# Masked-autoencoder loss: the first four target columns by three transfers in place of two

## The chip, the cores and the metric

The kernel runs on one core of one Trainium2 chip. The metric is the device time of one execution in microseconds (us). Of several executions the median is given, and one execution is taken by the hardware profiler. In the profile PE is TensorE (matrix multiply), PEld its weight loads, DVE is VectorE, ACT is ScalarE, POOL is GpSimd and SP is SyncE. SP and POOL issue the transfers here (DMA); 16 DMA engines move the data.

## The reference

There are 32 images of 147 masked patches, each patch with 768 numbers, in `pred` and in `target`, both float32. Each target patch is normalised by its own mean and variance, and the mean squared difference to the prediction is taken for each image.

```python
mean = target.mean(axis=-1, keepdims=True)
var = target.var(axis=-1, keepdims=True)
target = (target - mean) / np.sqrt(var + 1e-6)
loss = np.mean((pred - target) ** 2, axis=-1)   # (32, 147)
return loss.mean(axis=-1)                        # (32,)
```

## The kernel before

**Tiling.** Partition `p = 4 b + j` holds a run of consecutive patches of image `b`: `j` runs from 0 to 3 and picks one of four runs of 37 patches (36 real ones in the last run, `KJ` = 37, `KM` = 36). A "column" `c` is one patch of each partition, 128 x 768 numbers. Columns 0 to 35 exist on all 128 partitions. Column 36, called `REST`, exists only for three of the four runs and is a tile of 96 partitions. Since the patches of one run lie one behind the other in memory, a transfer of columns 0 to 3 moves one contiguous piece of 4 x 768 x 4 = 12,288 bytes for each partition.

**Loads.** A list `stream` names all loads in the order in which they are wanted. Columns 0 to 3 of the target and then `REST` of the target are marked `hw`: SP issues them, and they stay float32. All other pieces are marked `sw`: POOL issues them, and they are cast to bfloat16 on the way. Target and prediction pieces alternate in the POOL queue. Each tile is used once, so no load waits for a buffer; but a load from POOL reuses the completion semaphore of the load eight places before it and waits for that one. The function `load` (line 111 for the changed transfers, line 115 for all others) issues one entry of the list. The tile of columns 0 to 3 is filled by two transfers of 64 partitions: one takes the even partitions (`til[0::2]`, the runs `j` = 0 and 2), the other the odd ones.

**Work on a column.** VectorE computes the statistics of a target column (`bn_stats` twice for 384 numbers each, line 165, and `bn_aggr`, line 166). For a group of one to four columns ScalarE takes the root of the variance and the negative mean (lines 189 and 190), and VectorE the reciprocal (line 195). POOL then normalises the column into a bfloat16 tile `s` (line 215). The difference is either made on TensorE, by adding -1 x `s` and 1 x `pred` in PSUM with identity matrices (line 232), and squared with a sum on ScalarE (line 261); or it is made on VectorE (line 277) and squared there (line 281) or on ScalarE (line 261). At the end small matmuls with masks (line 342) add the partial sums of the partitions of each image into `acc`, which is copied (line 373) and stored (line 374).

**Order.** The order on each engine is written out by a planner in the kernel: it keeps a list of operations with an engine, an estimated duration, needs and earliest times, and picks the next one greedily. It works at build time and knows a load only as one operation on SP or POOL of 0.6 us; how many transfers `load` makes of it is not visible to it. The issue instructions are pinned in program order. The engines then run by semaphores alone.

Of the kernel before, what the change touches and what calls it, by code (L numbers as in the profile page):

```python
# [14 lines left out]
def kernel(  # L15
# [8 lines left out]
    pin = tc.keep_in_program_order  # L24
    B, N, D = pred.shape
    eps = 1e-6
    P = 128
    J = P // B
    KJ = (N + J - 1) // J
# [10 lines left out]
    def rows_of(c):  # L40
        return RP if c == REST else P
# [59 lines left out]
    def load(kind, c0, c1, d0, d1, q):  # L101
        x = targ_f if kind == "t" else pred_f
        n, w = rows_of(c0), d1 - d0
        til = data.tile([P, (c1 - c0) * w], BF16 if q == "sw" else F32, name=f"{kind}{c0}_{d0}")
        src = bass.AP(tensor=x.tensor, offset=x.offset + c0 * D + d0,
                      ap=[[N * D, B], [KJ * D, J - 1 if c0 == REST else J], [1, (c1 - c0) * w]])
        eng = {"hw": nc.sync, "hw2": nc.scalar, "sw": nc.gpsimd}[q]
        if c0 == 0 and q == "hw":

            for j in (0, 1):  # L110
                pin(eng.dma_start(out=til[j::2], in_=bass.AP(  # L111
                    tensor=x.tensor, offset=src.offset + j * KJ * D,
                    ap=[[N * D, B], [2 * KJ * D, J // 2], [1, (c1 - c0) * w]])))
        else:
            pin(eng.dma_start(out=til[:n], in_=src))  # L115
        for c in range(c0, c1):
            KIND[kind].setdefault(c, []).append((d0, d1, til, (c - c0) * w))
# [3 lines left out]
    for i, (kind, c0, c1, d0, d1, q) in enumerate(stream):  # L121
        w = (c1 - c0) * (d1 - d0)
        clock += w * rows_of(c0) / P * 0.915 / D + (0.0 if w >= 4 * D else 0.04)
        lanes[q].append(clock + 1.1)
        for c in range(c0, c1):
            land[kind, c, d0] = clock + 1.1
        k = len(lanes[q])
        op(("load", i), {"hw": "SP", "hw2": "ACT", "sw": "POOL"}[q], 0.6, [], lambda a=stream[i]: load(*a), rank=-1.0,
           early=0.0 if k <= 8 else lanes[q][k - 9] + 0.3)
# [164 lines left out]
    for k, (u, d0, d1, eng) in enumerate(units):  # L294
        w = len(u) * (d1 - d0)
# [40 lines left out]
        out=rl_sum, in_=rl, axis=mybir.AxisListType.X, op=ALU.add)), rank=3.0)  # L336
# [73 lines left out]
```

## Time and profile before

| | us |
|---|---|
| median of 4 runs | 76.79 |
| lowest and highest | 76.45, 77.25 |
| the profiled execution | 76.45 |
| its span, first to last instruction | 74.7 |

| engine | busy us | share of the span |
|---|---|---|
| VectorE | 55.9 | 75% |
| GpSimd | 52.6 | 70% |
| ScalarE | 31.0 | 41% |
| TensorE | 26.9 | 36% |

The POOL queue moved 13.52 MB as the profile counts them (bytes written, which are half the bytes read because of the cast), SP's queue 1.87 MB. The times in the profile's views are microseconds from the start of the span. A line number is that of the kernel before. In the chain of work that ended last, each entry names what the next one was released by; "SPq" is the sequencer of SP, and "issue" is time in which nothing shown was waited for. In a table of stretches, each engine's busy time is followed by its number of instructions, and the last columns are the granted TensorE clock, the mean busy share of the 16 DMA engines and the rate in GB/s. A transfer is counted in the stretch where its packets start, so a share can be over 1.

### The profile page before, as it was taken

How to read it: one execution, taken by the hardware profiler on the slowest of the kernel's cores; microseconds unless marked ns; L12 is line 12 of the kernel's file. 1: busy time of each engine (PE TensorE's matmuls, PEld its weight loads, DVE VectorE, ACT ScalarE, POOL GpSimd, SP SyncE). 2: the span in 40 equal slices, each digit the busy share in tenths (PEclk: the TensorE clock that was granted, in tenths of full speed). 3: DMA queues.
4: the chain of work that ended last, by engine and by line, in shares of the span. 5: the costliest groups of instructions: out<-in, count | busy, mean ns of one | idle time of the engine just before them, and what ended most of it. 6: DMA issues, size and time to landing. Idle time of an engine off the chain costs nothing.

```text
span 74.7 us, 563 instructions
## 1 busy us (share of the span) xinstructions
PE 26.9 (36%) x88; PEld 8.2 (11%) x88; DVE 55.9 (75%) x154; ACT 31.0 (41%) x67; POOL 52.6 (70%) x72
## 2 busy tenths in 40 slices
PE   0000003470000000498940004978860720578750
PEld 0000000110000000123300001222320300112120
DVE  0000899999999979990899999860997579999870
ACT  5100022202002020069502020598969979988960
POOL 5899008996199929699869993994799799960000
PEclk9999999999999999999999855589999998555895
DMA  0899999999999999999999989999999999999900
GB/s 0 191 428 355 260 217 214 195 223 224 240 217 210 210 198 211 234 217 210 230 217 224 217 185 214 211 217 214 217 214 220 197 212 212 215 204 206 168 1 0
DMA packets 3269, 15.41 MB, mean 206 GB/s; under 512 B 386, under 2 KB 1122, under 8 KB 2754
## 3 DMA queue, kind: packets, MB, share of 16 engines
q0 software_dynamic: 2992, 13.52, 88.7%
q1 hardware_dynamic: 274, 1.87, 7.0%
q14 instruction: 3, 0.02, 0.1%
HBM read 28.90 MB, written 0.00 MB: 387 GB/s over the span
## 4 chain that ended last, share of the span: by engine, by line
DMA 72%; DVE 10%; POOL 10%; issue 2%; ACT 1%; PE 1%; SPq 1%; ACTq 0%; POOLq 0%; DVEq 0%
DMA p<-in_pred_dram 63%; POOL s L215 9%; DMA t<-in_target_dram 8%; DVE st L165 6%; DVE zd L277 2%; DVE mv L166 1%; SPq L111 1%; ACT zp L261 1%; POOL p L115 1%; PE zp L232 1%; PE acc L342 0%; ACT r L189 0%; DVE ob L373 0%; DVE r L195 0%; ACTq L405 0%
## 5 line engine op out<-in xcount | busy, mean ns | idle before, releaser
L215 POOL TENSOR_SCALAR s<-t,nm,r 128x768 bf16<-128x768 bf16 (+2 forms) x37 | 39.2, 1066 | 6.9 <-DVE r L195 6.4
L165 DVE BATCH_NORM_STATS2 st<-t 128x6 f32<-128x384 bf16 (+2 forms) x74 | 36.2, 530 | 8.1 <-DMA t<-in_target_dram 8.1
L232 PE MATMUL z<-p,ident 128*128 128x512 bf16 (+2 forms) x26 | 9.5, 504 | 21.7 <-DMA p<-in_pred_dram 21.7
L189 ACT ACTIVATE r<-mv,eps_t 128x4 f32<-128x4 f32 (+2 forms) x11 | 3.2, 295 | 31.0 <-DVE mv L166 30.2
L261 ACT ACTIVATE z<-z 128x1536 f32<-128x1536 f32 (+1 forms) x9 | 12.3, 1364 | 8.1 <-PE z L232 8.1
L232 PE MATMUL z<-s,nident 128*128 128x512 bf16 (+2 forms) x26 | 10.1, 504 | 15.2 <-POOL s L215 13.9
L115 POOL DMA_DIRECT2D p<-in_pred_dram x15 | 8.6, 572 | 6.1 <-DMA t<-in_target_dram 4.1
L277 DVE TENSOR_TENSOR zd<-p,s 128x1536 bf16<-128x1536 bf16 (+4 forms) x13 | 8.7, 689 | 2.0 <-DMA p<-in_pred_dram 1.8
L166 DVE BATCH_NORM_AGGREGATE mv<-st 128x2 f32<-128x12 f32 (+1 forms) x37 | 7.7, 209 | 1.3
L232 PEld LDWEIGHTS <-ident 128*128 128x128 bf16 (+1 forms) x36 | 4.4, 122 | 35.6 <-issue 34.0
L261 ACT ACTIVATE zd<-zd 128x1536 bf16<-128x1536 bf16 (+1 forms) x5 | 6.7, 1348 | 0.7 <-DVE zd L277 0.5
L232 PEld LDWEIGHTS <-nident 128*128 128x128 bf16 (+1 forms) x36 | 3.4, 111 | 27.3 <-issue 14.9
L281 DVE SCALAR_TENSOR_TENSOR zd<-zd 128x512 bf16<-128x512 bf16 (+3 forms) x8 | 5.4, 680 | 0.2
L195 DVE RECIPROCAL r<-r 128x4 f32<-128x4 f32 (+2 forms) x11 | 1.5, 133 | 4.0 <-ACT r L189 4.0
L232 PE MATMUL zp<-p,ident 128*128 128x512 bf16 x5 | 2.4, 561 | 4.8 <-DMA p<-in_pred_dram 4.8
L115 POOL DMA_DIRECT2D t<-in_target_dram x6 | 3.6, 624 | 0.0
L261 ACT ACTIVATE zl<-zl 128x512 f32<-128x512 f32 (+1 forms) x5 | 2.8, 563 | 0.4 <-PE zl L232 0.3
L261 ACT ACTIVATE zp<-zp 128x1024 f32<-128x1024 f32 (+1 forms) x3 | 2.6, 865 | 0.3 <-PE zp L232 0.2
L232 PE MATMUL zp<-s,nident 128*128 128x512 bf16 x5 | 1.6, 427 | 2.5 <-ACT z L261 2.5
L232 PE MATMUL zl<-p,ident 128*128 128x512 bf16 (+1 forms) x5 | 2.2, 500 | 0.7 <-DMA p<-in_pred_dram 0.7
L232 PE MATMUL zl<-s,nident 128*128 128x512 bf16 (+1 forms) x5 | 1.9, 420 | 0.4 <-POOL s L215 0.4
L190 ACT ACTIVATE nm<-mv 128x4 f32<-128x4 f32 (+2 forms) x11 | 2.1, 189 | 0.0
(29 smaller groups left out, 10.7 us busy)
## 6 DMA issues: line engine op xcount, KB each, us to landing
t<-in_target_dram POOLq DMA_DIRECT2D x4, 768.0 KB, 13.4
t<-in_target_dram POOLq DMA_DIRECT2D x2, 1536.0 KB, 27.1
p<-in_pred_dram POOLq DMA_DIRECT2D x4, 768.0 KB, 38.4
t<-in_target_dram SPq DMA_DIRECT2D x2, 768.0 KB, 5.5
p<-in_pred_dram POOLq DMA_DIRECT2D x1, 1536.0 KB, 39.0
p<-in_pred_dram POOLq DMA_DIRECT2D x4, 384.0 KB, 29.9
p<-in_pred_dram POOLq DMA_DIRECT2D x3, 192.0 KB, 15.7
t<-in_target_dram SPq DMA_DIRECT2D x1, 288.0 KB, 8.1
```

The lines of the kernel that those rows point to most:

```text
L111: pin(eng.dma_start(out=til[j::2], in_=bass.AP(tensor=x.tensor, offset=src.offset + j * KJ * D, ap=[[N * D, B], [2 * KJ * D, J // 2], [1, ...
L115: pin(eng.dma_start(out=til[:n], in_=src))
L165: pin(nc.vector.bn_stats(out=st[:n, j, :], in_=x))
L166: pin(nc.vector.bn_aggr(out=out, in_=st[:n, :len(parts)]))
L189: pin(nc.scalar.activation(out=r[:n], in_=mv[:n, :, 1], func=ACTF.Sqrt, bias=eps_t[:n], scale=1.0))
L190: pin(nc.scalar.activation(out=nm[:n], in_=mv[:n, :, 0], func=ACTF.Copy, scale=-1.0))
L195: pin(nc.vector.reciprocal(out=rs[g][:n], in_=rs[g][:n]))
L215: pin(nc.gpsimd.tensor_scalar(out=s[:n, so:so + D], in0=til[:n, o:o + D], scalar1=nm, scalar2=r, op0=ALU.add, op1=ALU.mult))
L232: pin(nc.tensor.matmul(z[:n, zo + a:zo + b], eye[:n, :n], src[:n, o + a:o + b], start=first, stop=not first))
L261: pin(nc.scalar.activation(out=z[:n, :w], in_=z[:n, :w], func=ACTF.Square, accum_out=dest[:n]))
L277: pin(nc.vector.tensor_tensor(out=x, in0=y, in1=v, op=ALU.subtract))
L281: pin(nc.vector.scalar_tensor_tensor(out=z, in0=z, scalar=1.0, in1=z, op0=ALU.mult, op1=ALU.mult, accum_out=dest))
```

## The change

The tile of columns 0 to 3 is filled by three transfers: 32 partitions (every fourth, from 0: run `j` = 0), then 64 partitions (the odd ones: runs 1 and 3), then 32 partitions (every fourth, from 2: run `j` = 2). Each partition is still one piece of 12,288 bytes, and the tile, its consumers and all other loads are unchanged. SP issues the three transfers and then `REST`, four in place of three. The consumers of the tile (line 165 on VectorE and line 215 on POOL) wait for three completion semaphores in place of two.

```diff
         if c0 == 0 and q == "hw":
 
-            for j in (0, 1):
-                pin(eng.dma_start(out=til[j::2], in_=bass.AP(
+
+            for j, step in ((0, 4), (1, 2), (2, 4)):
+                pin(eng.dma_start(out=til[j::step], in_=bass.AP(
                     tensor=x.tensor, offset=src.offset + j * KJ * D,
-                    ap=[[N * D, B], [2 * KJ * D, J // 2], [1, (c1 - c0) * w]])))
+                    ap=[[N * D, B], [step * KJ * D, J // step], [1, (c1 - c0) * w]])))
```

The change adds one line to the file, so lines after it have a number higher by one in the kernel after.

## The prediction

> **What bounds the kernel now.** I read the chain that ended last first, then the page's slices and totals, then stretches of the trace at the start and at the end, and last the instructions of the first microseconds.
>
> The chain that ended last, merged, in order of time (start us, us, what):
>
> ```profile
> 0.81 0.63 SPq L111
> 1.45 0.06 issue
> 1.50 6.16 DMA t<-in_target_dram
> 7.66 0.03 issue
> ...
> 16.57 39.92 DMA p<-in_pred_dram
> ...
> 63.61 7.46 DMA p<-in_pred_dram
> 71.07 0.04 issue
> 71.12 0.39 PE zp L232
> ...
> 72.59 0.18 DVE ob L373
> ```
>
> The reader is to see that 72% of the chain is DMA, and that its head is the pair of transfers that is changed: the second is issued at 1.45 and lands at 7.66, and only then does VectorE begin. From this alone one would say that the start of VectorE sets the end, and that is the reading to distrust. The page says what the transfer engines did meanwhile:
>
> ```profile
> DMA  0899999999999999999999989999999999999900
> HBM read 28.90 MB, written 0.00 MB: 387 GB/s over the span
> ```
>
> They are 90% busy or more from the third slice to the thirty-eighth. The stretches at both ends (columns: five engines, granted clock, DMA share, GB/s written):
>
> ```profile
> 2.00:2.20 0.20, 0.00 (x0) 0.06 (x1) 0.00 (x0) 0.09 (x1) 0.17 (x1) 1.00 0.00 0
> 2.20:2.40 0.20, 0.00 (x0) 0.00 (x0) 0.00 (x0) 0.00 (x0) 0.13 (x2) 1.00 3.44 614
> ...
> 4.00:6.00 2.00, 0.00 (x0) 0.00 (x0) 0.00 (x0) 0.00 (x0) 2.00 (x5) 1.00 0.96 406
> ...
> 68.00:70.00 2.00, 2.00 (x6) 0.56 (x5) 1.82 (x8) 1.77 (x6) 0.00 (x0) 0.58 1.16 204
> 70.00:71.00 1.00, 0.47 (x2) 0.10 (x1) 0.86 (x5) 0.88 (x5) 0.00 (x0) 1.00 0.93 134
> 71.00:72.00 1.00, 0.82 (x13) 0.38 (x12) 0.93 (x4) 0.94 (x3) 0.00 (x0) 1.00 0.02 2
> ```
>
> Data first moves at 2.2 and stops at 71.1: 68.9 us for 28.90 MB, 419 GB/s, next to 406 GB/s in the stretch 4 to 6, where plain f32 copies alone run (GpSimd's transfers write bf16, so half of what they read). The stream never pauses for long, so the end is the moment its first byte moves, plus a fixed amount of work, plus 3.6 us of tail. VectorE's head can slip without moving the end so long as GpSimd issues its transfers early enough: its last issue, at 66.01, lands some 5 us later behind transfers already queued. VectorE itself waits 0.52 us at 27.85 and 0.78 us at 49.18 for target data, and 2.0 us twice for ScalarE. So what the change is worth is what it does to the start of the stream.
>
> **What the Trainium skill says.** "DMA: Bandwidth & Descriptors", Why a DMA increments its semaphore by 16 and not by 1: the engines used are the largest number up to 16 that divides the slowest dimension of both access patterns. 64 rows and 32 rows both give 16, four rows and two rows to an engine; the 406 GB/s agrees for 64, and no run yet shows 32. Same page, Queues, rings and completion order: an engine alternates between the queues that have work, packet by packet. The trace agrees: SP's transfers have the engines alone at first (406 GB/s), then the written rate falls to 316 in 6 to 8 and to 240 in 8 to 10, when GpSimd's come in. Same page, Rules for kernel authors: two transfers to disjoint halves of the partitions share the same engines and run one after the other; by this a third gains no bandwidth. Same page, Latency and other measured facts: first byte after about 0.6 us for this path; here the first data moves 1.4 us after the issue begins at 0.81, or 0.8 after it ends.
>
> **The change part by part.**
>
> ```profile
> 0.81 1.27 SPq L111 DMA_DIRECT2D t<-in_target_dram  x2
> 2.13 0.61 SPq L115 DMA_DIRECT2D t<-in_target_dram  x1
> 3.10 1.24 POOL L115 DMA_DIRECT2D t<-in_target_dram  x2
> ...
> 7.76 1.02 DVE L165 BATCH_NORM_STATS2 st<-t 128x6 f32<-128x384 f32 x2 [6.82 <-DMA t<-in_target_dram]
> ```
>
> (1) One more issue on SP. A 64-row issue takes 0.58 or 0.63 us and the 96-row one 0.61; only the single row of the output takes less (0.29). So the price hardly follows the rows, and a 32-row issue is taken at 0.6: the three start near 0.81, 1.4 and 2.05, and the transfer of the last column group (line 115), queued behind them on SP, moves from 2.13 to 2.7. SP has nothing else until the output. GpSimd's queue is not touched: its first issue stays at 3.10.
>
> (2) The same 128 rows of 12,288 bytes in a new order. At 406 GB/s over 16 engines a row takes 0.48 us. The packet records show 0.46 in steady flow, and 0.85 to 1.34 for each engine's very first row. Bytes and rows per engine (8) are as before, so the flow costs nothing more. The added semaphore writes, one per engine, take 0.01 us each in those records.
>
> (3) Does the ring run dry behind a first transfer of only two rows per engine? First data at 2.23, two rows of about 1.1 and 0.46: needed again at 3.8. The second transfer is issued at 1.4 and, with the same 1.42 us to first data, is ready at 2.85: 0.95 us early. The third, issued at 2.05, is ready at 3.5 and needed at 3.8 + 4 x 0.46 = 5.6. The last group: ready at 4.1, needed at 6.5, when the before trace's first rows of it move. All three are covered by data in flight; the loss is 0. If the cover were gone, each late 0.1 us would be 0.1 us at the end, since the stream bounds it.
>
> (4) The start of the first data. This is the one term that can move the end. With everything fixed per instruction the gain is 0. The upper end: the output's one row needs about 0.73 us from issue to its packet, against 1.42 for the 64 rows; if all 0.69 of the difference were in proportion to the rows, half the rows would save 0.35. Issues of 64 and 96 rows cost the same, which speaks for the fixed kind, so I take 0.1.
>
> (5) The waits. VectorE's first statistics and GpSimd's first normalisation wait for three semaphores in place of two; a queue step of this kind is 0.02 us in the chain, and behind VectorE's wait stands its whole sequence, which has slack as shown. The order of instructions on VectorE, ScalarE, TensorE and GpSimd is the same, because the planner sees one load as before.
>
> The sum: 0.1 off the stream's start, some 0.02 on the wait, so 0.1 off the end. The profiled execution took 76.45 us for a span of 74.7, so 76.35 for it; that execution was the lowest of the four, 0.34 under their median of 76.79, and against the median the forecast is 76.7.
>
> **The rivals.**
> A, the forecast: no change, 76.7. For it: equal bytes, equal engines, all later transfers ready early, and an end bound by the stream.
>
> B, an early start: the first data moves 0.35 sooner because half as many rows have to be described before it. For it, the difference between the output's 0.73 and 1.42. Against it, 0.58 to 0.63 for 64 rows and 0.61 for 96. Time 76.79 - 0.35 = 76.4. It would take 0.77 us to leave the band of 1%, and the GpSimd transfers, which first move near 7.0 whatever SP does, would leave a hole if SP's work ended early.
>
> C, slower: the ring runs dry after the first two rows per engine. What the trace gives for the second transfer is only a latest time of readiness: its rows follow the first's without a pause, at 2.23 + 1.1 + 3 x 0.46 = 4.7. If they were ready only then, say because descriptors of successive transfers are made one after the other, the engines would stand idle from 3.8 to 4.7, and the end would come 0.9 later: 77.7. It decides from the point where the second transfer needs over 2.4 us from issue to data, in place of the 1.42 that the first took. Against it: all rows of the first followed each other without a gap, so making them keeps ahead of moving them.
>
> D, the change doesn't do what it says: 32 rows use only 8 engines. These would carry 4 + 4 + 4 rows, four more than now, 4 x 0.48 = 1.9 us, and the end follows the fullest engine: 78.7. Against it stands the rule on the number of engines named above.
>
> **How the numbers follow.** A 0.62, B 0.17, C 0.16, D 0.05. One per cent is 0.77 us, about what a measurement of this kernel can tell from no change; the four runs before lie within 0.80 of each other. Faster by over 1%: a fifth of B and 0.03 of A, 0.05. Slower by over 1%: half of C, all of D, 0.05 of A, 0.16. Within it: 0.79. The range: A with the 0.4 that a median of a few runs can be off, and B's end, gives 76.1 below; above, 77.6 takes in most of C and leaves D out.
>
> **What would show it.** Right: SP's four issues of about 0.6 each and the last at 2.7; first data between 2.0 and 2.3 and no stretch without data after it up to 5 us; VectorE's first statistics between 7.4 and 7.8; the last data near 71.0. A first issue of 0.3 and first data before 1.95 would be B. A stretch of 0.4 us or more with no data between 3 and 5 us would be C. First data on fewer engines and VectorE starting near 9 would be D. I am wrong altogether if the front is as forecast and the last data still comes 0.8 us earlier or later than 71.1: then the end hangs on something between 8 and 60 us that I called slack.

## The result: slower by 0.8%, and the profile after

| | us |
|---|---|
| before, median of 59 runs | 76.62 (76.30 to 77.47) |
| after, median of 38 runs | 77.27 (76.82 to 77.94) |
| ratio | 1.0082, 95% interval 1.0064 to 1.0100 |
| the profiled execution after | 77.25, span 75.6 (76.45 and 74.7 before) |

One run of the kernel after, in a slower state at 78.00, is left out. The sign of the loss is certain; its size lies just inside the 1% band. In the trace after, SP and VectorE at the front (start us, us, engine, line):

```profile
0.81 1.85 SPq L112 DMA_DIRECT2D t<-in_target_dram  x3
...
2.71 0.63 SPq L116 DMA_DIRECT2D t<-in_target_dram  x1
...
8.90 1.02 DVE L166 BATCH_NORM_STATS2 st<-t 128x6 f32<-128x384 f32 x2 [7.96 <-DMA t<-in_target_dram]
```

The issues are where they were forecast (0.58 to 0.63 us each, the last at 2.71). VectorE begins at 8.90 in place of 7.76, against a forecast of 7.4 to 7.8. The profile's lines on transfers (the busy share of the transfer engines in forty slices of the span, in tenths, and the bytes read):

```profile
DMA  0899999999999999999999999999999999999700
HBM read 28.90 MB, written 0.00 MB: 383 GB/s over the span
```

The same bytes in the same dense band, and yet 383 for 387 GB/s. Where the front lost is seen in half-microsecond stretches, first the kernel before, then after (last two columns: DMA share and GB/s written, both counted where a packet starts):

```profile
5.50:6.00 0.50, 0.00 (x0) 0.00 (x0) 0.00 (x0) 0.00 (x0) 0.50 (x2) 1.00 0.93 393
6.00:6.50 0.50, 0.00 (x0) 0.00 (x0) 0.00 (x0) 0.00 (x0) 0.50 (x3) 1.00 0.92 393
6.50:7.00 0.50, 0.00 (x0) 0.00 (x0) 0.00 (x0) 0.00 (x0) 0.50 (x3) 1.00 0.82 320
```

```profile
5.50:6.00 0.50, 0.00 (x0) 0.00 (x0) 0.00 (x0) 0.00 (x0) 0.50 (x2) 1.00 1.41 393
6.00:6.50 0.50, 0.00 (x0) 0.00 (x0) 0.00 (x0) 0.00 (x0) 0.50 (x3) 1.00 0.64 270
6.50:7.00 0.50, 0.00 (x0) 0.00 (x0) 0.00 (x0) 0.00 (x0) 0.50 (x3) 1.00 0.93 270
```

A share of 1.41 at an unchanged 393 GB/s means that the packets which start there take longer, not that there are more of them. The next stretch then starts fewer, 270 in place of 393. The packet records name the packets: nine rows of the third transfer (a row is the piece of one partition, one packet), each the first on its engine, take 0.69 to 1.12 us in place of 0.46, and they start at 5.50 to 5.94, just behind the second transfer. Beyond 0.46 that is 3.7 us in all, 0.23 for each of the 16 engines on average and 0.66 on the worst. On four engines the row behind it then has to take turns with GpSimd's packets, and the last of the 128 rows ends at 7.97 in place of 7.16. By bytes moved, counted over all engines, the stream after is 0.18 us ahead of before at 5.5 us and 0.16 behind at 9, and it stays 0.2 behind until 70 us. No later work gives it back.

The end (the same two stretches that were shown of before):

```profile
70.00:71.00 1.00, 0.98 (x4) 0.30 (x3) 0.90 (x7) 0.80 (x4) 0.00 (x0) 0.50 1.06 161
71.00:72.00 1.00, 1.00 (x10) 0.28 (x9) 0.97 (x5) 0.75 (x3) 0.00 (x0) 0.67 0.14 17
```

The last data comes at 71.41 in place of 71.13, and from there to the end of the span it takes 4.1 us in place of 3.6. The second part goes with TensorE's clock in this one execution. Granted clock by slices, before and then after:

```profile
PEclk9999999999999999999999855589999998555895
```

```profile
PEclk9999999999999999999998555559999999655598
```

A half-speed stretch lies later in the profiled execution after, and covers the last matmuls (clock 0.50 and 0.67 in the two stretches above; 0.98 and 1.00 us of TensorE busy in place of 0.47 and 0.82). The chain that ended last runs over TensorE:

```profile
6.92 39.16 DMA p<-in_pred_dram
46.08 0.04 issue
46.12 1.45 PE z L233 x3
...
68.45 1.79 PE zl L233 x4
70.23 0.02 issue
70.25 0.92 PE zl L233 x2
```

Ahead of the last matmuls the chain runs over GpSimd, from 59.45 to 67.8, and GpSimd's last issue comes at 67.77 in place of 66.01. The stream did not wait for it: in each microsecond from 67 to 70 it writes 198 to 212 GB/s after and 202 to 206 before. Runs with a low and with a high mean clock occur with both kernels, so the runs can be compared at equal clock (the runs before are those taken beside the experiments). With a mean granted clock of 0.94 to 0.951 the median is 76.52 before (56 runs) and 77.06 after (14 runs); with 0.88 to 0.892 it is 76.97 (35) and 77.62 (14). Half a microsecond or more of the 0.65 stays at equal clock. The one trace after shows 0.28 of it as later data; where the rest arises at equal clock is not shown.

### The profile page after: what moved, and what is told of

Its sections match the earlier page's. It is cut to its first block, busy times and chain, and to the rows that moved or that the text cites. A ratio compares the mean times of both kernels' runs of the same rounds, so it can differ in the third digit from the quotient of the medians.

```text
span 75.6 us, 565 instructions
## 1 busy us (share of the span) xinstructions
PE 26.0 (34%) x88; PEld 8.2 (11%) x88; DVE 56.6 (75%) x154; ACT 30.7 (41%) x67; POOL 53.4 (71%) x72
## 4 chain that ended last, share of the span: by engine, by line
DMA 52%; POOL 15%; PE 12%; DVE 8%; ACT 4%; POOLq 3%; issue 2%; ACTq 0%
DMA p<-in_pred_dram 52%; POOL s L216 7%; PE z L233 7%; POOL t L116 4%; PE zl L233 4%; DVE st L166 4%; POOLq L406 3%; DVE zd L278 3%; ACT z L262 2%; POOL p L116 2%; ACT zl L262 1%; ACT zp L262 1%; PE zp L233 1%; DVE mv L167 1%; POOL nident L144 0%
## 5 line engine op out<-in xcount | busy, mean ns | idle before, releaser
L216 POOL TENSOR_SCALAR s<-t,nm,r 128x768 bf16<-128x768 bf16 (+2 forms) x37 | 39.9, 1086 | 9.1 <-DVE r L196 8.6
L233 PE MATMUL z<-s,nident 128*128 128x512 bf16 (+2 forms) x26 | 9.2, 458 | 17.3 <-POOL s L216 15.0
L278 DVE TENSOR_TENSOR zd<-p,s 128x1536 bf16<-128x1536 bf16 (+4 forms) x13 | 9.2, 723 | 0.4 <-DMA p<-in_pred_dram 0.4
L282 DVE SCALAR_TENSOR_TENSOR zd<-zd 128x512 bf16<-128x512 bf16 (+3 forms) x8 | 6.0, 753 | 0.2
```

Source lines behind the costliest of these rows:

```text
L216: pin(nc.gpsimd.tensor_scalar(out=s[:n, so:so + D], in0=til[:n, o:o + D], scalar1=nm, scalar2=r, op0=ALU.add, op1=ALU.mult))
L233: pin(nc.tensor.matmul(z[:n, zo + a:zo + b], eye[:n, :n], src[:n, o + a:o + b], start=first, stop=not first))
L278: pin(nc.vector.tensor_tensor(out=x, in0=y, in1=v, op=ALU.subtract))
L282: pin(nc.vector.scalar_tensor_tensor(out=z, in0=z, scalar=1.0, in1=z, op0=ALU.mult, op1=ALU.mult, accum_out=dest))
```

## The experiments

The diffs show the lines that matter; a tile or a list that they need is made elsewhere in the kernel. Two theories stood at first. H: VectorE's late start sets the loss. S: only the stream of transfers does.

**1. VectorE later, transfers unchanged (head2).** From the kernel before:

```diff
+        if g[i] == 0:
+            for _ in range(2):
+                pin(nc.vector.bn_stats(out=extra, in_=til[:n, o:o + half]))
         bn(mvs[g][:n, i], ...)
```

> The kernel before, with two more statistics instructions of 384 numbers on VectorE directly ahead of the first real ones, after the same wait; their result is not used. All transfers are as before; VectorE's sequence begins about 1.06 us later (2 x 0.53), about as late as in the changed kernel (8.9 in place of 7.76). Theory H, VectorE's late head sets the loss: slower by 0.5 to 0.7 us, ratio 1.007 to 1.009, as the changed kernel. Theory S, only the stream of transfers matters (0.2 us behind in the changed kernel): no change, ratio 0.999 to 1.002, the delay is absorbed in VectorE's waits near 28 and 36 us.

Measured: 76.56, ratio 0.9999 (0.9974 to 1.0024).

```profile
7.96 1.16 DVE L178 BATCH_NORM_STATS2 extra<-t 128x6 f32<-128x384 f32 x2 [7.01 <-DMA t<-in_target_dram]
9.03 1.00 DVE L166 BATCH_NORM_STATS2 st<-t 128x6 f32<-128x384 f32 x2
```

The real statistics begin at 9.03, later than in the changed kernel, and it costs nothing. H falls. The 8.90 that strikes the eye first in the profile after is not what costs time.

**2. GpSimd's queue later (three_swlate).** From the changed kernel, in `masks`, ahead of GpSimd's first transfer:

```diff
     def masks():
+        for _ in range(6):
+            pin(nc.gpsimd.memset(late, 0.0))
```

> The changed kernel, with six memsets of 128 x 128 on GpSimd ahead of its first transfer, so that GpSimd's queue comes in about 1.2 us later. Theory H with a collision (the last rows of the third transfer share their engines with GpSimd's queue from 6.6 us on): VectorE's first statistics come back to 7.7 to 8.0 and the time falls to 76.6 to 76.9, ratio to before 1.000 to 1.004. Theory S or a cause inside SP's queue: VectorE's start stays near 8.9 or falls only by the doubled packets; GpSimd's later start leaves the engines empty for up to 0.5 us, and the time is 77.3 to 77.8.

Measured: 77.91, ratio 1.0168 (1.0131 to 1.0205); GpSimd's first issue at 4.56, VectorE at 9.31, last data at 72.77. That is a little over the second branch. Taking GpSimd's queue away from the front makes it worse, so sharing the engines with it is not what costs. The third transfer's rows are late as in the changed kernel (single rows up to 1.41 us), and less is there to fill the gap. The kernel before was not run with this delay; there GpSimd's packets do not move until 6.99 us in any case.

**3. One transfer of 128 (one128).** `til[:n]` in a single transfer, from the kernel before.

> The kernel before, with one transfer of 128 partitions for columns 0 to 3 in place of two, so that one fewer issue stands ahead of the last column group on SP. If each added transfer costs (its issue, its first rows that take 0.7 to 1.1 us in place of 0.46): VectorE starts at 7.2 to 7.6 and the time is 0.2 to 0.5 us less, ratio 0.994 to 0.997. If the transfers' number isn't the cause, only their order against GpSimd's queue: VectorE's start 7.6 to 8.0, ratio 0.999 to 1.003; first data later than 2.3 if the descriptors of 128 rows take longer than those of 64.

Measured: 76.58, ratio 1.0009 (0.9986 to 1.0032), VectorE at 7.95, first data at 2.2. This is the second branch: one transfer fewer gains nothing, so transfers do not cost by the piece. One or two ahead of the last group are free, three are not.

**4. Other orders of the three (order_32_32_64, order_64_32_32).**

```diff
-            for j, step in ((0, 4), (1, 2), (2, 4)):
+            for j, step in ((0, 4), (2, 4), (1, 2)):
```

> The changed kernel with the two transfers of 32 first and that of 64 last. If the slow first rows of a transfer that begins late (5.5 us in the changed kernel) are the cause: the last transfer begins at about 4.7, its four rows per engine run at 0.46 each unless GpSimd's queue is near, so VectorE starts at 7.6 to 8.0 and the ratio to before is 1.000 to 1.004. If the number of transfers or SP's fourth issue is the cause: as the changed kernel, VectorE at 8.5 to 9, ratio 1.006 to 1.010.

Measured: 78.33, ratio 1.0230 (1.0200 to 1.0260), last data at 72.66. Neither branch: slower than both. With two small transfers ahead, the third is wanted from 4.4 us on, and of its rows single ones take up to 1.26 us; the last of the 128 ends at 9.44, and VectorE starts at 10.30.

The other order, `((1, 2), (0, 4), (2, 4))`:

> The changed kernel with the transfer of 64 first, then the two of 32. What is left after the first runs: the loss is in the stream, not in VectorE's head; the third transfer on SP's queue is not ready when the engines want it. Theory R1, SP's transfers become ready one after the other, some 1.5 us apart, whatever their size: the third is ready between 4.5 and 6 and wanted at 5.6, the fourth at 6.7 and wanted at 6.6; a small loss, ratio 1.002 to 1.007. Theory R5, the third becomes ready only some 2 us after the first has completed: the first completes at 4.7 to 5.3, so the third's rows come at 6.7 to 7.3, about 1.2 us late; ratio 1.012 to 1.025. Theory R0 of the forecast (a fixed 1.4 us from issue to data): ratio 1.000.

Measured: 77.38, ratio 1.0110 (1.0061 to 1.0159), last data at 71.82. R0 falls; R5 as stated too, since the late rows start at 5.2 to 6.0 and end by 7.1, where it had them come at 6.7 to 7.3. R1's ratio is missed a little.

**5. More transfers, more rows (four32, three128).** Four steps of 4, `((0, 4), (1, 4), (2, 4), (3, 4))`; and thirds of each partition's piece:

```diff
+            third = (c1 - c0) * w // 3
+            for k in range(3):
+                pin(eng.dma_start(out=til[:, k * third:(k + 1) * third], in_=bass.AP(
+                    tensor=x.tensor, offset=src.offset + k * third,
+                    ap=[[N * D, B], [KJ * D, J], [1, third]])))
```

> Columns 0 to 3 by four transfers of 32 partitions (every fourth partition each), then the last column group as the fifth on SP. Each needs two rows per engine, so each is wanted 0.92 us after the one before. R1 (1.5 us apart whatever the size): the third's first rows near 4.6 to 6, the fourth's near 6.7, the last group near 8; the engines run dry three times until GpSimd's queue comes in; the stream is over 1 us behind at 9 us, ratio 1.020 to 1.035. R2 (ready in proportion to the rows): 64 rows stand ahead of the third as in the order 32, 32, 64, so the third as there, the fourth with 96 ahead at 5.6 to 6.5; ratio 1.010 to 1.025. R0: all ready in time, ratio 1.000.

> Columns 0 to 3 by three transfers of all 128 partitions, each with a third of every partition's piece (4,096 bytes): as many transfers as in the changed kernel, three times the rows. R1 or R5 (what counts is the number of transfers): as the changed kernel, ratio 1.004 to 1.012, VectorE's start between 8 and 9. R2 (time for each row): 128 rows stand ahead of the second and 256 ahead of the third in place of 96, so the second comes near 6 us and the third near 10; ratio 1.03 to 1.06. R0: ratio 1.000 to 1.003.

Measured: four32 77.86, ratio 1.0168 (1.0124 to 1.0211); three128 78.16, ratio 1.0195 (1.0142 to 1.0249). A cost for each row (R2) falls: with 256 rows ahead the third came at 5.2 to 6.6, no later than with 96, and not near 10. R1 and R5 miss three128's ratio, and four32 is below R1's 1.020; it lies in R2's range, which three128 rules out. All five runs of four32 had a clock near 0.886, where the kernel before has 76.97, so part of its ratio can be the clock. In three128 the first column lies in the first third, so VectorE began at 4.75, three microseconds early, and the kernel was still 2% slower: an early head did not save it.

**6. The fourth off SP's queue (three_rest_act).** From the changed kernel:

```diff
-    piece("t", REST, REST + 1, q="hw")
+    piece("t", REST, REST + 1, q="hw2")
```

> The changed kernel with the last column group's target issued by ScalarE's queue at its start in place of fourth on SP. Its data then comes in at 2 to 3 us among the first rows, so the third transfer is wanted about 0.8 us later, at 6.3, and no fourth is on SP. R1 with a queue for each issuer: no row waits, ratio 0.997 to 1.002. R1 with one maker for both issuers: the third on SP is then the fourth in all, ready at 6.7 or later; ratio 1.006 to 1.015. If the three transfers cost by themselves (their strides, their semaphores): ratio 1.006 to 1.010 as the changed kernel.

Measured: 76.75, ratio 1.0018 (0.9991 to 1.0045), last data at 71.32, although VectorE starts at 8.79. The records show the last group's rows, now in ScalarE's queue, moving from 3.6 to 4.8, between SP's first and second transfer; no row of SP's third takes longer than 0.6 us. The same third transfer, wanted a microsecond later (from 6.6 us on in place of 5.5), is in time; so its rows are not slow by themselves, and the long packets of the changed kernel are read as rows that are not there when the engines are free. The run is not free of loss: beside the last group's rows, 20 rows of the second transfer take 0.59 to 0.77 us, and the stream is 0.2 us behind before from 5.5 us on. The profiled execution took 76.64 in place of 76.45, which fits that lag.

**7. GpSimd's queue earlier (three_swearly, two_swearly).** If that is so, other rows should fill the hole. The two masks are made behind GpSimd's first eight transfers in place of ahead of them (the line that made them ahead is emptied, which is not shown):

```diff
         else:
             pin(eng.dma_start(out=til[:n], in_=src))
+        if q == "sw":
+            first_sw.append(c0)
+            if len(first_sw) == 8:
+                masks()
```

> The changed kernel, with the making of the two masks moved behind GpSimd's first eight transfers, so that GpSimd's queue begins 1.1 us earlier (near 2.0 in place of 3.1). If the loss comes from engines that wait at 5.5 to 6.6 us for rows of SP's third and fourth transfers, GpSimd's rows fill the hole: the last data comes at 71.1 or earlier, ratio to before 0.997 to 1.003, though VectorE's head gets later still (9 or more). If the loss comes from sharing the engines with GpSimd's queue, it grows: ratio 1.010 to 1.020.

> The kernel before with the same move of the masks. It has no hole at the front, so an earlier queue of GpSimd fills nothing: ratio 0.998 to 1.002 if holes are what counts. VectorE's head gets later, since the last rows of columns 0 to 3 share the engines from about 5.5 on; by the head2 run that costs nothing up to 1 us. If sharing is what costs: ratio 1.005 or more.

Measured: with three transfers 76.57, ratio 0.9996 (0.9971 to 1.0020); with two 76.58, ratio 1.0022 (0.9989 to 1.0056). The changed kernel with this move:

```profile
1.84 1.24 POOL L117 DMA_DIRECT2D t<-in_target_dram  x2
...
9.59 0.56 DVE L171 BATCH_NORM_STATS2 st<-t 128x6 f32<-128x384 f32 x1 [8.65 <-DMA t<-in_target_dram]
```

and its stretch from 71 to 72 us:

```profile
71.00:72.00 1.00, 0.81 (x13) 0.38 (x12) 0.92 (x4) 0.94 (x4) 0.00 (x0) 1.00 0.00 0
```

GpSimd issues at 1.84 in place of 3.10, VectorE starts at 9.59, later than in the changed kernel, and no data is left to move after 71.0: the last comes at 71.00. The whole loss is gone, also at equal clock (76.49 in seven runs with 0.94 to 0.951). This is the decisive pair with run 2: GpSimd 1.5 us later, 1.7% slower than before; 1.3 us earlier, level with it. It does not beat the kernel before; there the same move gains nothing either.

**8. Why the rows are late: the spacing by itself (measure32, measure128).** Columns 0 to 3 by four small transfers and two larger ones; forty memsets hold GpSimd back to 13.5 us:

```diff
+            for i, (j, step, e0, e1) in enumerate([(0, 4, 0, 1536), (1, 4, 0, 1536), (2, 4, 0, 1536),
+                    (3, 4, 0, 1536), (0, 2, 1536, 3072), (1, 2, 1536, 3072)]):
+                pin(eng.dma_start(out=til[j::step, e0:e1], ...))
```

(measure128: the list `(0, 1, 0, 384)`, `(0, 1, 384, 768)` and so on, all partitions.)

> The spacing by itself: columns 0 to 3 by four transfers of 32 partitions with 6,144 bytes each (two rows per engine, about 0.46 us of data), then two of 64 partitions for the rest, then the last column group, all on SP. Forty memsets hold GpSimd's queue back by about 10 us, so that nothing else uses the engines; the time is therefore no measure. SP issues every 0.6 us. R0 of the forecast (fixed 1.4 us from issue to data): the transfers' first packets stand 0.6 us apart. R1 (ready one after the other, slower than they are issued): they stand 1.0 to 1.6 us apart, with empty engines between them.

> The same with all 128 partitions in each of the four first transfers and 1,536 bytes per partition (8 rows per engine, about 0.5 us of data), the same bytes per transfer. R1 (a time for each transfer): the same spacing as with 32 partitions, within 0.3 us. R2 (a time for each row): up to four times the spacing, 4 us or more if it was 1.0 to 1.6. R0: 0.6 us.

Measured: the completions of the first four transfers (median of the engines' semaphore writes) at 3.0, 3.6, 4.35 and 4.95 us with 32 partitions; 3.1, 3.8, 4.45 and 5.05 with 128. They stand 0.6 to 0.75 us apart, as they are issued. R1 falls for transfers of this size: preparing them one by one is not slow, neither by transfer nor by row.

**9. With the real sizes, alone on the engines (three_hold, two_hold, four_hold, measure32_free).** The same forty memsets in the changed kernel, the kernel before and four32; and measure32 without them.

> The changed kernel with forty memsets ahead of GpSimd's first transfer, which then starts near 13 us, so that SP's four transfers have the engines alone (the time is no measure). The measured spacing of small transfers fell to about 0.65 us, so preparing them one by one isn't what makes the third late. Theory G (GpSimd's making of descriptors from 3.1 us on holds up SP's): no row of the third transfer takes over 0.6 us, VectorE starts at 7.2 to 7.7. Theory B (SP's ring is fed late when two transfers are already under way): first rows of the third still take 0.7 to 1.1 us on about half of the engines, VectorE starts at 8 or later.

> The control: the kernel before with the same forty memsets. Its third transfer on SP is the last column group. Both theories: rows of columns 0 to 3 at 0.46 us, VectorE at 7.2 to 7.8. Theory B: the last group's rows of 3,072 bytes, third on SP and wanted at 6.5, take over 0.12 us for the first of each engine; theory G: all 0.12.

> The same hold with four transfers of 32 and the last group fifth. Theory G: rows at 0.46 us throughout, all 128 rows done by 7.2. Theory B: the third's first rows, wanted at 4.6, and the fourth's, wanted at 5.5, come late on many engines, and the 128 rows are done at 8 or later.

> The measurement of small transfers (four of 32 partitions with 6,144 bytes, two of 64, the last group) without the hold[...]. Theory G: the third and fourth transfer, which came at 3.7 to 5.2 us with the hold, come at least 0.7 us later now. Theory B: they come as with the hold, within 0.3 us, and only rows from 5.5 us on differ, where GpSimd's rows share the engines.

Stretches of three_hold and then of two_hold:

```profile
5.50:6.00 0.50, 0.00 (x0) 0.00 (x0) 0.00 (x0) 0.00 (x0) 0.41 (x2) 1.00 1.04 246
6.00:6.50 0.50, 0.00 (x0) 0.00 (x0) 0.00 (x0) 0.00 (x0) 0.41 (x2) 1.00 0.78 295
```

```profile
5.50:6.00 0.50, 0.00 (x0) 0.00 (x0) 0.00 (x0) 0.00 (x0) 0.41 (x2) 1.00 0.98 418
6.00:6.50 0.50, 0.00 (x0) 0.00 (x0) 0.00 (x0) 0.00 (x0) 0.40 (x2) 1.00 0.84 356
```

With nothing but SP's transfers on the engines, three of them move at 246 and 295 GB/s where two move at 418 and 356. In three_hold 13 rows of the third transfer take 0.62 to 1.28 us and VectorE starts at 8.41; in two_hold no row of columns 0 to 3 that starts after 3.2 us takes over 0.6, and VectorE starts at 7.29. In four_hold 13 first rows of the third transfer, wanted from 4.4 on, take 0.97 to 1.54 us, and the fourth's then take 0.46 to 0.64; VectorE at 8.77. In measure32_free the third and fourth complete at 4.3 and 5.0, as with the hold. (Its single run took 79.39: with seven transfers on SP the stream is 1.4 us behind before from 16 to 70 us.) Theory G falls: the lateness is there when only SP's queue is at work. B stands in the main, with two misses: in four_hold the fourth transfer is not late, and in two_hold the first rows of the last group, third on SP, start at 6.36 and take 0.12 us; single later rows take up to 0.19. Where the first rows of the third transfer are late, they end between 5.1 and 7.1 us in the kernels with full pieces, three to five microseconds after its issue near 2.05, while a third small transfer took 2.3 us from issue to completion.

Why a third transfer behind two full ones is fed late is not settled. A fixed latency, a time per transfer, a time per row and GpSimd's activity were tried and fell. A limit on what one queue may have under way is a guess that is not shown: the wait after the first transfer's completion is not the same in these runs.

**All full-size kernels side by side:**

| kernel | stream behind before at 16 us, us | last data, us | ratio to before |
|---|---|---|---|
| three_swearly | -0.18 | 71.00 | 0.9996 |
| two_swearly | -0.06 | 71.08 | 1.0022 |
| before | 0 | 71.13 | 1 |
| head2 | -0.15 | 71.15 | 0.9999 |
| one128 | -0.11 | 71.18 | 1.0009 |
| three_rest_act | 0.20 | 71.32 | 1.0018 |
| after | 0.20 | 71.41 | 1.0082 |
| four32 | 0.48 | 71.73 | 1.0168 |
| order_64_32_32 | 0.29 | 71.82 | 1.0110 |
| order_32_32_64 | 0.72 | 72.66 | 1.0230 |
| three128 | 0.98 | 72.72 | 1.0195 |
| three_swlate | 0.81 | 72.77 | 1.0168 |

The first two columns are of one profiled execution each, so single places may swap. Before and the five kernels level with it have their last data by 71.32, the six slower ones later. The lag is counted in bytes over all sixteen engines. What it is at 16 us it still is at 70, within 0.02 us, in every one of these kernels: between the two nothing is made up and nothing more is lost. The last data can come later than that mean says, because the engines do not all end together: in order_32_32_64 the packets of the sixteen end between 70.5 and 72.7, in the kernel before between 70.4 and 71.1.

## Why the prediction was wrong

The forecast was 76.7, 0.1 us faster than before, with a range of 76.1 to 77.6. It came 0.65 us slower. The median of 77.27 lies in the range only because room was left above for rival C, and that room was worked out for another transfer than the one that was late.

- **What bounds the kernel: right, and shown.** The stream sets the end (of its "90% busy or more" one slice, the twenty-fourth, is at 8 tenths), and VectorE's head can slip: 1.3 us of slip costs 0.0% (run 1), and a lag of the front is still there at 70 us.
- **(1) Issues: right.** 0.58 to 0.63 us each, the last at 2.71.
- **(2) Flow: right for rows that are there.** 0.46 us each in steady flow.
- **(3) Does the ring run dry: the step that failed.** Its sum "The third, issued at 2.05, is ready at 3.5 and needed at 3.8 + 4 x 0.46 = 5.6" carried the first transfer's 1.42 us from issue to data over to the third, and the loss was set at 0. The second was in time in the main, as forecast. The third was not: it was wanted from 5.5 us on, and its rows took up to 0.66 us longer than 0.46, 0.23 on average over the engines, in the profiled execution. The price taken at nothing is these 0.2 us in the stream there; filling the hole (run 7) takes back the whole loss of about half a microsecond at equal clock. The step itself said what a missing cover costs, and the sentence "each late 0.1 us would be 0.1 us at the end" held for the stream: what the front lost was still missing at 70 us. That the time lost is more than the stream's mean lag is not accounted for in full.
- **(4) Start: right in size.** First data at 2.17 in place of 2.23, 0.06 earlier where 0.1 was taken.
- **(5) Waits: right in that they cost nothing at the end.** VectorE starts 0.93 us after the last of the 128 rows, in place of 0.60; by run 1 such a delay is absorbed.
- **Rival C had the right kind of loss at the wrong place.** It put the dry ring behind the first transfer and priced it at 0.9; the late one was the third. The sign named for C, a stretch of 0.4 us without data between 3 and 5 us, did not appear. The evidence against C, that the first transfer's own rows follow each other without a gap, spoke about rows inside one transfer and not about the next but one. The trace before gave only a latest time for the third (the last column group, at 6.5), and 5.6 lies ahead of it: that was the bound to keep open.
- **Rival D falls.** VectorE's start near 9 was named as its sign, but the records hold 64 completion writes for SP's four transfers, sixteen for each, so those of 32 rows use all sixteen engines.
- **A sentence under B was wrong.** "GpSimd transfers, which first move near 7.0 whatever SP does": in measure32_free, with the same issue at 3.10, they moved at 4.8. In the kernel before they first move when an engine is through with its SP rows; "packet by packet" describes what happens from 7 us on. Since a third transfer is late, GpSimd's rows are what can fill the gap, and the forecast overlooked that.

## What to carry to other kernels

In these kernels, where the stream of transfers sets the end, a hole at its front is still missing at the end; ask of each transfer on a queue, not only of the first, when its rows can be there, and take as proven only what the trace shows of a transfer at the same place in its queue. Splitting a load into more transfers on one queue moves that question to rows that nobody has yet seen waiting. Do not call an engine's late start a loss until a delay put there on purpose costs time.

## What was not expected of the hardware

- A third transfer of full pieces on SP's queue can be late: its late first rows end three to five microseconds after its issue (at 5.1 to 7.1 us, issue near 2.05), where the first transfer has its first data 1.4 us after its issue. The first four small transfers of measure32 and measure128 do not show it (completions 0.6 to 0.75 us apart).
- The late rows of the changed kernel and its like show as long packets, 0.6 to 1.5 us in place of 0.46, and not as idle engines: the profile's DMA row after stays at 9 there.
- GpSimd's packets move at 4.8 us in measure32_free, but with the same issue at 3.10 they first move at 6.99 in the kernel before, when an engine is through with its share of SP's 128 rows; from then on the two queues take turns.
